# Four quarters for the last rows of a feed-forward's way down, and one low part by subtraction

## The chip, the cores and the metric

The kernel runs on one core of a Trainium2 chip. The metric is the device time of one execution in microseconds (us), the median of several runs. Engines: TensorE (PE) multiplies, VectorE (DVE) and ScalarE (ACT) work on tiles, GpSimd (POOL) issues adding transfers, SyncE (SP) issues the loads.

## What is computed

A trunk of two layers works on 512 rows of 1024 features. The first layer holds an mLSTM mixer, the second a gMLP mixer. Each mixer stands between two half-step feed-forwards (SwiGLU, hidden width 2816), and each layer ends with a gated embedding ("ple").

```python
def swiglu_ffn(x, w_gu, w_d):
    g, u = jnp.split(x @ w_gu, 2, axis=-1)
    return (jax.nn.silu(g) * u) @ w_d
...
x = layer_norm(DN_ALPHA * x + 0.5 * swiglu_ffn(x, ffn1_wgu[i], ffn1_wd[i]), ln_g[i, 0], ln_b[i, 0])
```

So there are four feed-forwards in a run, called here **A** (before the mLSTM), **B** (before the first ple), **C** (before the gMLP) and **D** (before the last ple).

## The kernel before

Float32 products are made of three products of a reduced type. Every operand is split into a high part (`hi`, a rounded copy) and a low part (`lo`, what the copy lost), and `mm3` (L388 to L390) multiplies hi by hi, hi by lo and lo by hi. A weight's high part is made by ACT (L275). Its low part comes in one of two ways: DVE subtracts (L284 at once; L290 later, "apart", inside a feed-forward), or ACT writes minus the weight (L281) and a POOL transfer adds the weight onto it (L282). Which forms take the second way is set by `by_dma`.

The class `Weights` (L50 to L360) holds the order in which weights are used. Loads go into three slots of 1 MB (`wraw`). A slot can serve as a box of two halves of 512 KB (`wbox`). `load` issues the next transfer as soon as a slot or a half is free, `fill` splits the next weights as soon as a tile for them is free. In a feed-forward `fill` leaves a weight alone that was only just loaded:

```python
if self.apart and self.ready and self.loaded_at[j] > self.clock - 2:
    return meanwhile
```

A feed-forward works through the 22 blocks of its hidden width in chunks of 2, 4, 4, 4, 4 and 4. From the third chunk on, two blocks of the way up are computed as seven products (a Strassen-like scheme). `up_forms` makes the seven weight forms r0 to r6 in place, in the boxes. r5 is the sixth. Tiles `ups` are the sums of the way up, `gps` those of the earlier chunks' way down. The last chunk's way down (`dps`, in the function `down`) needs four rows of `wd`, of 128 by 1024 each, called here rows 0 to 3. For each of four token tiles (t = 0 to 3) TensorE runs over the four rows, two halves of 512 columns and three products. DVE then adds each half to the residual (L763), takes statistics (L726 to L732) and normalises (L740, or L744 and L746). Meanwhile ACT and DVE split the normalised tile for the next stage (`xh` L639, `xl` L640), once TensorE has transposed it (`xps` L631).

The next stage begins straight behind: `sup` products of the mLSTM behind A, `pwp` of the ple behind B and D, `gvps` of the gMLP behind C. The first two weights of that stage are called n1 and n2 here. Their loads stand behind the rows' loads in SP's queue, and their splits behind the rows' splits.

Before, `add_rows` (L514) loads the four rows as two loads of 1 MB, each of two rows. The kinds in its list name the pools that the split rows take ("main", "rows", "rowsx").

Of the kernel before, what the change touches and what calls it, by code (L numbers as in the profile page):

```python
# [44 lines left out]
PLE_EXTRA = 3  # L45
UP_BY_DMA = (1, 3, 4, 5, 6)
UP_BY_DMA_2 = (1, 3, 5, 6)


class Weights:  # L50
# [307 lines left out]
def hybrid_trunk(ctx: ExitStack, tc, x, p, ln_g, ln_b, ffn1_wgu, ffn1_wd, ffn2_wgu, ffn2_wd,  # L358
# [82 lines left out]
    W = Weights(nc, raw_pool, split_pool)  # L441
# [4 lines left out]
    def kp(w):  # L446
        return w.rearrange("(kb p) c -> p kb c", p=P)
# [4 lines left out]
    def add_pairs(w, a0, b0):  # L452

        W.add((w_cols(w, a0), cols2), (w_cols(w, b0), cols2))

    def kinds_of(kind, at):
        return kind if isinstance(kind, str) else kind[at:at + 2]

    def add_rows(w, kb, n, kind="main"):
        for k in range(0, n, 2):  # L460
            W.add((kp(w)[:, kb + k:kb + k + 2, :], rows2), kind=kinds_of(kind, k))
# [9 lines left out]
    LAST = len(FFN_CHUNKS) - 1  # L471
# [3 lines left out]
    def ffn_weights(wgu, wd, name, ple=False):  # L475
        starts = [sum(FFN_CHUNKS[:c]) for c in range(LAST + 1)]

        def forms(c):
            m = FFN_CHUNKS[c] // 2

            def quarter(i, j):
                k = starts[c] + m * i
                return kp(wd)[:, k:k + m, j * 512:(j + 1) * 512]
            loads = [W.add_load(quarter(i, j), n, name) for i, j, n in ((0, 0, 2), (0, 1, 1), (1, 1, 1), (1, 0, 2))]
            return W.forms("rows", *((j, slice(None)) for j in loads))

        first = len(W.order)
        for at in range(starts[UP_FROM]):
            if at == 0 or at == starts[UP_FROM] - 1:
                W.add(*((kp(wgu)[:, :, c0:c0 + P], [slice(None)]) for c0 in (at * P, HID + at * P)))  # L490
            elif at % 2:
                add_pairs(wgu, at * P, HID + at * P)
        tiles = W.order[first:]
        del W.order[first:]
        for c, n in enumerate(FFN_CHUNKS):
            down_w = deque(forms(c - 1) if c else ())
            if c >= UP_FROM:
                products = []
                for b in range(starts[c], starts[c] + n, 2):
                    products += W.up_forms(*(W.add_load(kp(wgu)[:, k:k + 4, c0:c0 + 2 * P], 1, "box")  # L500
                                             for c0 in (b * P, HID + b * P) for k in (0, 4)),
                                            by_dma=UP_BY_DMA if b == starts[c] else UP_BY_DMA_2)
                for s, product in enumerate(products):
                    W.order.append(product)
                    if s % 2:
                        W.order.append(down_w.popleft())
                continue
            for i in range(2 * n):
                W.order.append(tiles[2 * starts[c] + i])
                if down_w:  # L510
                    W.order.append(down_w.popleft())
        if ple:
            W.add_hook("rows", lambda hi, lo: turn_p.pop()(hi, lo))
        add_rows(wd, starts[LAST], 4, ["rowsx", "rows", "main", "main"] if ple else ["main", "rows", "rowsx", "rows"])  # L514


    ML_SLOTS = (2, 3, 4, 5, 6, 7, 11)
# [71 lines left out]
    def ple_weights(i):  # L589
        add_rows(ple_wp[i], 0, 2)  # L590
        add_wide(ple_wg[i], 0, ["extra", "extra", "extra", "main"])
        add_wide(ple_wg[i], 512, ["rows", "rows", "rowsx", "rows2"])

    ffn_weights(ffn1_wgu[0], ffn1_wd[0], (0, 0))
    ml_weights()
    ffn_weights(ffn2_wgu[0], ffn2_wd[0], (0, 2), True)
    ple_weights(0)
    ffn_weights(ffn1_wgu[1], ffn1_wd[1], (1, 0))
    gm_weights()
    ffn_weights(ffn2_wgu[1], ffn2_wd[1], (1, 2), True)  # L600
# [1349 lines left out]
```

## Time and profile before

| what | value |
|---|---|
| runs | 2192.62, 2196.89, 2197.5 us; median 2196.89 |
| profiled execution | 2193.39 us, its span 2191.7 us |
| granted TensorE clock, mean | 0.999 |
| PE busy | 2170.3 us (99%) in 12821 matmuls |
| DVE busy | 1760.5 us (80%) |
| ACT busy | 1208.1 us (55%) |
| POOL busy | 226.3 us (10%) |

The span is the time from the first to the last record of the profiled execution. The rest of its time lies around it. TensorE is busy nearly all the time, so a change of the time is a change of what TensorE waits for, or of the rate at which it works. In the timeline an entry in brackets is the idle time of the engine before the instruction, and what ended it.

### The profile page before, as it was taken

The numbers are of one execution on the slowest core, as the hardware profiler recorded it, in microseconds if no ns is written. First come the engines' busy times: TensorE is split into PE (matmuls) and PEld (weight loads), VectorE is DVE, ScalarE is ACT, GpSimd is POOL, SyncE is SP. The second block draws the span as 40 slices with busy tenths as digits, with TensorE's granted clock in tenths as the row PEclk, the third lists the DMA queues.
The fourth block names the chain that finished last, engine by engine and source line by source line (L and its number), as shares of the span: only waits on it lengthen the run. The fifth ranks groups of instructions, "written<-read, shape, count | busy, mean of one in ns | idle before, by whom it ended". The sixth has DMA issues, their size and how long they took to land.

```text
span 2191.7 us, 32537 instructions
## 1 busy us (share of the span) xinstructions
PE 2170.3 (99%) x12821; PEld 1922.0 (88%) x12821; DVE 1760.5 (80%) x2532; ACT 1208.1 (55%) x1668; POOL 226.3 (10%) x279
## 2 busy tenths in 40 slices
PE   9999999999999999999999999999999999999998
PEld 8899997888888889999888899997888888999987
DVE  5898877786767789888887998877788679988887
ACT  4576656454546445667444566655345553666642
POOL 1011100011101101111000011110001100111100
PEclk9999999999999999999999999999999999999999
DMA  6587764366857426887531587754437743777651
GB/s 187 156 204 184 172 153 136 92 154 128 155 130 154 135 81 163 200 194 172 173 125 58 153 207 186 176 145 135 144 77 140 168 135 116 179 191 179 135 183 58
DMA packets 228097, 329.46 MB, mean 150 GB/s; under 512 B 9140, under 2 KB 163892, under 8 KB 227944
## 3 DMA queue, kind: packets, MB, share of 16 engines
q1 hardware_dynamic: 169104, 211.83, 29.8%
q0 software_dynamic: 52224, 100.86, 27.5%
q10 hardware_dynamic: 6616, 14.69, 1.9%
q8 instruction: 101, 1.65, 0.3%
q14 instruction: 52, 0.43, 0.1%
HBM read 224.58 MB, written 2.11 MB: 103 GB/s over the span
## 4 chain that ended last, share of the span: by engine, by line
PE 78%; DVE 11%; issue 4%; ACT 4%; DMA 3%; SPq 0%; POOL 0%; DVEq 0%; ACTq 0%; POOLq 0%
PE ups L390 7%; PE ups L388 7%; PE ups L389 7%; PE gps L388 6%; PE gps L389 6%; PE gps L390 6%; DMA wlo<-wbox 2%; PE dps L389 2%; PE dps L390 2%; PE dps L388 2%; DVE wlo L290 2%; PE fps L388 2%; PE fps L389 1%; PE fps L390 1%; ACT whi L275 1%
## 5 line engine op out<-in xcount | busy, mean ns | idle before, releaser
L275 ACT ACTIVATE whi<-wbox 128x1024 fp32r<-128x1024 f32 x224 | 235.7, 1054 | 242.2 <-DVE wbox L141 96.9
L390 PE MATMUL ups<-xh,wlo 128*128 128x256 f32 x1024 | 290.3, 284 | 3.2 <-DMA wlo<-wbox 3.2
L388 PE MATMUL ups<-xh,whi 128*128 128x256 f32 x1024 | 289.9, 283 | 0.0
L389 PE MATMUL ups<-xl,whi 128*128 128x256 f32 x1024 | 289.7, 283 | 0.0
L275 ACT ACTIVATE whi<-wraw 128x1024 fp32r<-128x1024 f32 (+1 forms) x212 | 217.3, 1046 | 96.7 <-DVE wraw L119 22.6
L388 PE MATMUL gps<-whi,fhi 128*128 128x512 f32 x644 | 253.0, 393 | 0.4
L389 PE MATMUL gps<-wlo,fhi 128*128 128x512 f32 x644 | 252.2, 392 | 0.0
L390 PE MATMUL gps<-whi,flo 128*128 128x512 f32 x644 | 251.4, 390 | 0.0
L282 POOL DMA_DIRECT2D wlo<-wbox x144 | 122.2, 848 | 1076.8 <-ACT wlo L281 705.0
L763 DVE TENSOR_TENSOR xt<-xt,gps 128x512 f32<-128x512 f32 x302 | 194.9, 680 | 26.7 <-PE gps L390 26.7
L284 DVE TENSOR_TENSOR wlo<-wraw,whi 128x1024 fp32r<-128x1024 f32 (+1 forms) x140 | 167.6, 1214 | 41.8 <-ACT whi L275 40.9
L390 PEld LDWEIGHTS ups<-xh,wlo 128*128 128x128 f32 x1024 | 196.2, 192 | 4.3 <-DMA wlo<-wbox 4.2
L388 PEld LDWEIGHTS ups<-xh,whi 128*128 128x128 f32 x1024 | 196.1, 192 | 3.8 <-ACT us L1085 1.6
L389 PEld LDWEIGHTS ups<-xl,whi 128*128 128x128 f32 x1024 | 196.1, 192 | 2.3
L275 ACT ACTIVATE whi<-wquarter 128x1024 fp32r<-128x1024 f32 (+1 forms) x140 | 135.3, 966 | 77.0 <-DVE wquarter L119 28.9
L281 ACT ACTIVATE wlo<-wbox 128x1024 fp32r<-128x1024 f32 x144 | 150.4, 1044 | 0.0
L390 PEld LDWEIGHTS gps<-whi,flo 128*128 128x128 f32 x644 | 120.9, 188 | 26.9
L388 PEld LDWEIGHTS gps<-whi,fhi 128*128 128x128 f32 x644 | 121.3, 188 | 23.9 <-issue 1.6
L389 PEld LDWEIGHTS gps<-wlo,fhi 128*128 128x128 f32 x644 | 121.3, 188 | 21.6
L944 DVE TENSOR_TENSOR flo<-h,fhi 128x512 fp32r<-128x512 f32 (+1 forms) x140 | 88.5, 635 | 57.6 <-ACT fhi L941 57.0
L290 DVE TENSOR_TENSOR wlo<-wquarter,whi 128x1024 fp32r<-128x1024 f32 x104 | 126.6, 1218 | 0.0
L388 PE MATMUL fps<-xh,whi 128*128 128x512 f32 x288 | 112.2, 390 | 0.0
(365 smaller groups left out, 5822.4 us busy)
## 6 DMA issues: line engine op xcount, KB each, us to landing
wlo<-wbox POOLq DMA_DIRECT2D x144, 512.0 KB, 5.8
wbox<-in_ffn_wgu_dram SPq DMA_DIRECT2D x128, 512.0 KB, 4.9
wquarter<-in_ffn_wd_dram SPq DMA_DIRECT2D x64, 512.0 KB, 5.8
wraw<-in_ml_w_in_dram SPq DMA_DIRECT2D x24, 1024.0 KB, 5.8
wlo<-wraw POOLq DMA_DIRECT2D x48, 512.0 KB, 6.4
wraw<-in_ffn_wgu_dram SPq DMA_DIRECT2D x15, 1024.0 KB, 6.0
wraw<-in_gm_w_in_dram SPq DMA_DIRECT2D x15, 1024.0 KB, 5.6
wraw<-in_ffn_wgu_dram SPq DMA_DIRECT2D x17, 512.0 KB, 4.8
```

The costliest lines, as they stand in the source:

```text
L275: self.nc.scalar.activation(hi[:, s], src[:, s], AF.Copy)
L281: self.nc.scalar.activation(lo[:, s], src[:, s], AF.Copy, scale=-1.0)
L282: self.nc.gpsimd.dma_start(lo[:, s], src[:, s], accum_op=OP.add)
L284: self.nc.vector.tensor_sub(lo[:, s], src[:, s], hi[:, s].bitcast(F32))
L290: self.nc.vector.tensor_sub(lo, src, hi.bitcast(F32))
L388: mm(ps, st[0], mv[0], start=start, stop=False, skip_group_check=more)
L389: mm(ps, st[0], mv[1], start=False, stop=False, skip_group_check=more)
L390: mm(ps, st[1], mv[0], start=False, stop=stop, skip_group_check=more)
L763: vec.tensor_add(dst, dst, ps)
L944: vec.tensor_sub(lo, src, hi.bitcast(F32))
```

## The change

The second pair of the last chunk makes r5's low part by subtraction on DVE. The four rows are loaded one by one, as halves of boxes. In a feed-forward that ends in a ple the second row's tile comes from the pool "main" and the third row's from "rows", the other way round than before.

```diff
+UP_BY_DMA_LAST = (1, 3, 6)
...
-                                            by_dma=UP_BY_DMA if b == starts[c] else UP_BY_DMA_2)
+                                            by_dma=UP_BY_DMA if b == starts[c] else UP_BY_DMA_2 if c < LAST else UP_BY_DMA_LAST)
...
-        add_rows(wd, starts[LAST], 4, ["rowsx", "rows", "main", "main"] if ple else ["main", "rows", "rowsx", "rows"])
+        for k, kind in enumerate(["rowsx", "main", "rows", "main"] if ple else ["main", "rows", "rowsx", "rows"]):
+            at = starts[LAST] + k
+            j = W.add_load(kp(wd)[:, at:at + 1, :], 1, "box")
+            W.order.append((kind, (j,), lambda j=j: (W.raws[j], (j,))))
```

The added lines shift the code: L290 of before is L291 of the change, L284 is L285, L740 is L744, L744 and L746 are L748 and L750, L763 is L767, L640 is L644, L1088 and L1104 are L1092 and L1108.

The order of TensorE's instructions stays as it was. Three places of DVE's order follow, before and then after.

The first place is the end of the last chunk in A, behind the last additions of `gps`. The three L290 are row 3, n1 and n2; the single L291 is row 3.

```order
L763 TENSOR_TENSOR xt<-xt,gps 128x512 x2
L290 TENSOR_TENSOR wlo<-wraw,whi 128x1024 x3
L763 TENSOR_TENSOR xt<-xt,dps 128x512
```

```order
L767 TENSOR_TENSOR xt<-xt,gps 128x512 x2
L291 TENSOR_TENSOR wlo<-wbox,whi 128x1024
L767 TENSOR_TENSOR xt<-xt,dps 128x512
```

The low parts of n1 and n2 are gone from this place. C changes here in the same way.

The second place is the end of the way down in A, from the statistics of the last token tile on, ahead of the mLSTM. Before, the four L284 are the weights behind n2.

```order
L730 BN_AGGR mv<-st 128x2
L732 TENSOR_SCALAR rs<-mv 128x1
L740 TENSOR_SCALAR xt<-xt,mv,rs 128x1024
L640 TENSOR_TENSOR xl<-xf,xh 128x4x128 x2
L284 TENSOR_TENSOR wlo<-wraw,whi 128x1024 x4
```

```order
L736 TENSOR_SCALAR rs<-mv 128x1
L744 TENSOR_SCALAR xt<-xt,mv,rs 128x1024
L285 TENSOR_TENSOR wlo<-wraw,whi 128x1024 x6
L644 TENSOR_TENSOR xl<-xf,xh 128x4x128 x4
```

The six L285 are n1, n2 and the four behind them, now ahead of the splits of x. In C the low parts of n1 and n2 go to a like place, one token tile sooner (behind the `xl` of t = 1, ahead of the L767 of t = 3).

The third place is B, from the gating of the last pair to the first addition of `dps` (D reads the same). Before, the single L290 is row 0, the five are rows 1, 2, 3, n1 and n2; after, the first two are rows 0 and 1, the second two rows 2 and 3.

```order
L1088 TENSOR_TENSOR us<-us,ups 128x512
L290 TENSOR_TENSOR wlo<-wraw,whi 128x1024
L1104 SCALAR_TENSOR_TENSOR us<-us 128x512
...
L763 TENSOR_TENSOR xt<-xt,gps 128x512 x2
L290 TENSOR_TENSOR wlo<-wraw,whi 128x1024 x5
L763 TENSOR_TENSOR xt<-xt,dps 128x512
```

```order
L1092 TENSOR_TENSOR us<-us,ups 128x512
L291 TENSOR_TENSOR wlo<-wbox,whi 128x1024 x2
L1108 SCALAR_TENSOR_TENSOR us<-us 128x512
...
L767 TENSOR_TENSOR xt<-xt,gps 128x512 x2
L291 TENSOR_TENSOR wlo<-wbox,whi 128x1024 x2
L767 TENSOR_TENSOR xt<-xt,dps 128x512
```

Here the low parts of n1 and n2 come behind the tile t = 2's L750, in a group of four L285 where before there was a group of two L284, ahead of the last tile's residual. ACT makes the high parts of n1 and n2 later as well, behind the splits of the second token tile (t = 1): in A in a group of six, ahead of the splits of t = 2 and t = 3, in B, C and D in a group of four where there was a group of two. Per feed-forward ACT has one instruction less (L281), POOL one adding transfer less (35 for 36), DVE one subtraction more. SP issues four loads of 512 KB where it issued two of 1 MB.

## Rows read from the trace of the kernel before

**Rows 1.** The waits of TensorE over the span: total, times, longest.

```profile
PE dps L389 <- DVE wlo L290: 4.8, 4, 1.6
PE ups L390 <- DMA wlo<-wbox: 3.9, 6, 1.0
PE sup L866 <- ACT xh L639: 1.1, 2, 0.8
```

**Rows 2.** The timeline of PE at the end of A: start, duration, what, idle before.

```profile
319.35 0.39 PE L390 MATMUL ups<-xh,wlo 128*128 128x256 f32 x1 [1.04 <-DMA wlo<-wbox]
...
333.92 0.50 PE L389 MATMUL dps<-wlo,wquarter 128*128 128x512 f32 x1 [1.60 <-DVE wlo L290]
...
353.97 0.28 PE L866 MATMUL sup<-xh,wlo 128*128 128x256 f32 x1
354.09 0.28 PE L866 MATMUL sup<-xh,whi 128*128 128x256 f32 x1
```

**Rows 3.** The timeline of DVE at the end of A.

```profile
322.29 0.69 DVE L1088 TENSOR_TENSOR us<-us,ups 128x512 f32<-128x512 f32 x1 [1.81 <-PE ups L390]
...
326.32 1.23 DVE L290 TENSOR_TENSOR wlo<-wraw,whi 128x1024 fp32r<-128x1024 f32 x1 [2.21 <-ACT whi L275]
...
332.64 3.49 DVE L290 TENSOR_TENSOR wlo<-wraw,whi 128x1024 fp32r<-128x1024 f32 x3
...
357.70 0.81 DVE L740 TENSOR_SCALAR xt<-xt,mv,rs 128x1024 f32<-128x1024 f32 x1 [0.66 <-POOL rs L733]
358.43 1.29 DVE L640 TENSOR_TENSOR xl<-xf,xh 128x512 fp32r<-128x512 f32 x2
```

**Rows 4.** The timeline of ACT in A: the third row's high part.

```profile
325.23 1.06 ACT L275 ACTIVATE whi<-wraw 128x1024 fp32r<-128x1024 f32 x1 [6.00 <-DMA wraw<-in_ffn_wd_dram]
```

**Rows 5.** The timeline of PE at the end of B.

```profile
1071.74 0.39 PE L390 MATMUL ups<-xh,wlo 128*128 128x256 f32 x1 [1.00 <-DMA wlo<-wbox]
...
1082.86 0.50 PE L389 MATMUL dps<-wlo,wquarter 128*128 128x512 f32 x1 [0.89 <-DVE wlo L290]
...
1105.00 0.39 PE L388 MATMUL pwp<-whi 128*128 128x512 f32 x1
1105.23 0.39 PE L389 MATMUL pwp<-wlo,whi 128*128 128x512 f32 x1
```

**Rows 6.** The timeline of DVE at the end of B.

```profile
1087.26 0.68 DVE L763 TENSOR_TENSOR xt<-xt,dps 128x512 f32<-128x512 f32 x1
...
1106.82 2.35 DVE L284 TENSOR_TENSOR wlo<-wraw,whi 128x1024 fp32r<-128x1024 f32 x2
```

**Rows 7.** The timeline of PE at the end of C.

```profile
1472.09 0.38 PE L390 MATMUL ups<-xh,wlo 128*128 128x256 f32 x1 [0.64 <-DMA wlo<-wbox]
...
1486.37 0.50 PE L389 MATMUL dps<-wlo,wquarter 128*128 128x512 f32 x1 [1.46 <-DVE wlo L290]
...
1506.08 0.39 PE L389 MATMUL gvps<-wlo,xh 128*128 128x512 f32 x1
```

**Rows 8.** The timeline of ACT at the end of C.

```profile
1505.59 1.04 ACT L275 ACTIVATE whi<-wraw 128x1024 fp32r<-128x1024 f32 x1
```

**Rows 9.** The timelines of PE and DVE at the end of D.

```profile
2126.32 0.39 PE L389 MATMUL pwp<-wlo,whi 128*128 128x512 f32 x1
2127.96 2.35 DVE L284 TENSOR_TENSOR wlo<-wraw,whi 128x1024 fp32r<-128x1024 f32 x2
```

**Rows 10.** The last matmul of the run, in the timeline of PE.

```profile
2182.95 0.28 PE L390 MATMUL gps<-whi,xl 128*128 128x256 f32 x1
```

**Rows 11.** Windows behind it: length, busy PE, PEld, DVE, ACT, POOL, PEclk, DMA, GB/s.

```profile
2184.00:2185.00 1.00, 0.00 (x0) 0.00 (x0) 0.79 (x2) 0.14 (x1) 0.00 (x0) 1.00 0.00 0
...
2186.00:2187.00 1.00, 0.00 (x0) 0.00 (x0) 1.00 (x3) 0.00 (x0) 0.85 (x1) 0.50 0.00 0
```

**Rows 12.** The timeline of PE at the start of the run.

```profile
1.43 3.36 PE L1903 MATMUL warm<-ident 128*128 128x128 f32 x16 [1.43 <-POOL ident masks.py:199]
4.91 1.09 PE L631 MATMUL xps<-ident,xt 128*128 128x128 f32 x8
```

## The prediction

> **What bounds the kernel now.** I read the times by engine first. TensorE is busy for 99% of the span, so there is no second engine whose load sets the end: time is gained or lost only where TensorE waits, or where its clock falls. The waits of TensorE come next, and they are few [rows 1]. Two of them touch what is changed: four waits of `dps` for a low part from DVE (4.8 us in all), and waits of `ups` for an adding transfer (six, 3.9 us, of which three are r5's). The timelines of the four feed-forwards then show what is late.
>
> In A, `ups` waits for r5's low part, which a POOL transfer adds up (1.04) [rows 2]. Fourteen microseconds on, `dps` waits for row 3's low part (1.60) [rows 2]. The reason lies on ACT: the high part of row 2 waits 6.00 us for the second load of two rows [rows 4]. Behind it ACT's `silu` of the last pair is held, and on DVE row 2's low part and the whole gating (326.32) [rows 3]. B has the r5 wait and a `dps` wait [rows 5], C has both [rows 7], D has the `dps` wait of B but no r5 wait.
>
> A wait takes more from TensorE than the bracket says, since the profile models a matmul's end. Matmuls of 256 columns start 0.12 apart and are drawn 0.28 long (the two `sup`) [rows 2], those of 512 columns start 0.23 apart and are drawn 0.39 long (the two `pwp`) [rows 5]; where one is drawn 0.50 long ahead of a `dps` wait, 0.27 is to be added. So a wait costs its bracket and 0.16, or 0.27 where I say so.
>
> **The change part by part.**
>
> *r5 by subtraction.* ACT loses one instruction of 1.05 and POOL one transfer per feed-forward; neither is waited for elsewhere. The waits go: 1.04 + 0.16 = 1.20 in A, 1.16 in B, 0.80 in C, nothing in D. DVE gets one subtraction of 1.22. It has an idle stretch of 1.81 just ahead of 322.29 [rows 3] to hide it; if that were gone, the gating would come 1.14 later.
>
> *Four quarters.* Rows 0, 1 and 2 no longer wait for a whole slot. In A the gating on DVE could then follow row 1's low part at once: row 2's starts at 322.29 + 0.69 + 1.22 = 324.20 at the latest where it was 326.32, 2.12 sooner, and all that follows with it. Row 3's low part, the first of the three at 332.64, ends at 332.64 − 1.20 − 2.12 + 1.22 = 330.54. TensorE will want it at 333.92 − 1.87 − 1.20 = 330.85. It is in time by 0.3 only. So 1.87 goes in A, and in the same way 1.46 + 0.16 = 1.62 in C. In B and D the first row that is late is row 1; it is now ready ahead of the gating, but that pushes the gating 1.14 back, and row 2's low part is late in its place: 1.16 goes and 0.89 comes, −0.27 each.
>
> *The first two weights of the next stage.* This is the part that speaks against the change. Before, the low parts of n1 and n2 were made right behind row 3's, some 20 us ahead of their use. A quarter's buffer comes free later than half of a load's did, the loads of n1 and n2 are issued later, and the rule that leaves a fresh load alone sends their splits past the whole way down. What is queued ahead of them on DVE is then the residual chain, and that chain ends when TensorE ends.
>
> - A. The low parts come behind the last normalisation (L740). That ends at 358.43 [rows 3]; less what was gained (1.20 + 1.87 = 3.07) it is 355.36, and n1's low part ends 1.22 later, at 356.58. TensorE wants it for the second matmul of `sup`, at 353.97 − 3.07 = 350.90. Loss 5.68. Two later waits of `sup` for the last token tile are swallowed by it: 1.1 [rows 1] and twice 0.16, 1.4.
> - B. DVE is free of three low parts, and is then held only by TensorE: the first half of `dps` of the first token tile is complete with the 13th matmul behind the one that waited, 1082.86 + 13 × 0.227 + 0.39 = 1086.20, less 0.27 is 1085.93, which is 1.33 ahead of 1087.26 [rows 6]. So DVE's chain comes 1.33 + 1.16 sooner. n1's low part then starts at 1106.82 − 2.49 = 1104.33 and ends at 1105.55. TensorE wants it at 1105.23 − 1.16 − 0.27 = 1103.80. Loss 1.75. n2 is wanted three matmuls later (0.68) and comes 1.14 later: 0.46 more. Together 2.21.
> - C. ACT's high part at 1505.59 [rows 8] is now n1's. Less 0.80 + 1.62 = 2.42 it ends at 1504.21, the low part 1.22 later at 1505.43, wanted at 1506.08 − 2.42 = 1503.66 [rows 7]. Loss 1.77; n2 has cover, since n1 serves many matmuls of `gvps`.
> - D. As B without the r5 gain: 2127.96 − 1.33 + 1.22 = 2127.85, wanted at 2126.32 − 0.27 = 2126.05 [rows 9]. Loss 1.80, and 0.46 for n2: 2.26.
>
> Sums: A −1.20 − 1.87 − 1.40 + 5.68 = +1.21; B −1.16 − 0.27 + 2.21 = +0.78; C −2.42 + 1.77 = −0.65; D −0.27 + 2.26 = +1.99. Together **+3.3**: 8.6 us of waits go, 11.9 come.
>
> *The clock.* In A TensorE would stand still for 5.7 us; no wait of [rows 1] is longer than 1.6. The trace shows what standing still does at one place: the last matmul of the run ends at 2183.23 [rows 10], the granted clock is still 1.00 at 2184 and 0.50 from 2186 on [rows 11], that is 1.2 GHz for 2.4. So it falls in less than three microseconds, and A's stall is long enough. What it then costs to come back is shown nowhere behind a fall. Below, it is nothing: the clock could be back with the first matmuls. The nearest row is the start of the run, where TensorE also comes from rest: 16 small matmuls in 3.36 (0.21 each) against 8 in 1.09 (0.14) just after [rows 12], 16 × 0.07 = 1.1 us. Above, I take as much as the stall itself, 5.7 us, as if half rate lasted for twice that. I take 1.1, the nearest row.
>
> The Trainium skill ("TensorE: Matmul & The Clock Gate", section "HAM oscillation — how this bites in real kernels") describes a kernel whose TensorE waits between bursts, falls to half rate, and pays at the head of each next burst. By that rule A's stall costs more than its length; without it the sum is +3.3, which is the first rival.
>
> The sum is +3.3 + 1.1 = **+4.4 us**. On the profiled execution (2193.39) that is 2197.8. This execution lies 3.5 below the median of the runs shown (2196.89), and the three runs spread over 4.9, so against the median the forecast is 2196.9 + 4.4 = **2201.3 us**. About 0.2% (4.4 us) is what a measurement of this kernel can tell from no change; the forecast lies on that line.
>
> **The rivals.**
>
> 1. *The stalls come, the clock holds or is back at once.* +3.3, 2200.2. For it: over the whole kernel the clock stays at 1.00. Against it: [rows 11].
> 2. *DVE's tail is not held by TensorE, and n1 is in time in B, C and D* (not slower). If the three low parts taken off DVE bring its chain 3 × 1.14 sooner right to the end, n1's low part in B ends at 1106.82 − 1.16 − 3.42 + 1.22 = 1103.46, ahead of 1103.80, and the like holds in D. It decides at that point: 1.8 us sooner than I reckon. Then B, C and D give −1.43, −2.42 and −0.27, and with A's +1.21 and 1.1 the sum is −1.8: 2195.1. Against it: `dps` halves cannot be added before TensorE has made them. Were A's stall gone as well, only the gains would stay, −8.6: 2188.3, clearly faster. For that n1's low part in A would have to come 5.7 us sooner, and it stands behind L740 on DVE.
> 3. *The quarters don't do what they are for.* If row 2's quarter also comes too late (it can be issued only once r3's adding transfer has read its buffer, and 0.3 us is all that row 3 has to spare), the waits of 1.87 and 1.62 stay in A and C. n1 is late there all the same: +4.4 + 3.5 = +7.9, 2204.8.
>
> **How the numbers follow.** I give the forecast 0.52, with the clock's price between 0 and 5.7 about it: 0.36 of this is slower by over 0.2%, 0.16 within. Rival 1 has 0.20 (within), rival 2 0.09 (within) and its faster end 0.07, rival 3 0.12 (slower). That is faster 0.07, same 0.45, slower 0.48. The range goes from rival 2 (2195.0) to the upper bound of the clock's price, 2196.9 + 3.3 + 5.7 = 2205.9, which takes in rival 3; the faster end is left out, and the spread of the runs about the ends.
>
> **What would show it.** Right: the `ups` waits of r5 and the `dps` waits of A and C are gone from TensorE's list, one wait of `sup` for a DVE low part of over 5 us stands in A, waits of `pwp` and `gvps` near 1.6 stand in B, C and D, and a granted clock below 1.00 appears behind A's stall. Wrong: the longest wait stays under 2 us; or n1's low part (L285) in A starts before L744; or the `dps` waits stay, which is rival 3. The forecast is wrong as a whole if those waits sum to less than the 8.6 that goes.

## The result, and the profile after

The change took 2200.07 us (median of 8 runs, 2198.12 to 2202.06), the kernel before 2194.68 (8 runs beside them). The ratio is 1.0025, 95% interval 1.0016 to 1.0035: slower by 5.4 us. The profiled execution of the change took 2199.77, with a span of 2198.1. The span is 6.4 us above that of before, a little more than the 5.4 between the medians.

The list of what TensorE waited for, over the whole span of the change (total, times, longest), answers to [rows 1]:

```profile
PE sup L870 <- DVE wlo L285: 5.4, 2, 5.1
PE pwp L390 <- DVE wlo L285: 3.7, 3, 1.8
PE dps L390 <- DVE wlo L291: 1.6, 2, 0.8
...
PE ups L391 <- DMA wlo<-wbox: 1.1, 3, 0.5
PE gvps L390 <- DVE wlo L285: 0.8, 1, 0.8
PE gvps L389 <- ACT whi L276: 0.7, 1, 0.7
```

The `dps` waits of A and C are gone, and r5's waits with them: the longest wait of `ups` is 0.5 where it was 1.0. In their place stand waits for the first weights of the next stage, 5.1 in A, 1.8 in each of B and D, and 0.7 + 0.8 in C.

The timeline of TensorE at the end of A, of the change, answers to [rows 2]. The first `sup` matmul goes, the second needs n1's low part:

```profile
351.50 0.38 PE L870 MATMUL sup<-xh,whi 128*128 128x256 f32 x1 [0.23 <-ACT whi L276]
356.95 0.58 PE L870 MATMUL sup<-xh,wlo 128*128 128x256 f32 x1 [5.07 <-DVE wlo L285]
357.33 0.41 PE L870 MATMUL sup<-xh,whi 128*128 128x256 f32 x1
357.55 0.41 PE L870 MATMUL sup<-xh,wlo 128*128 128x256 f32 x1
```

DVE at the same place answers to [rows 3]. Row 3's low part is made alone and in time; n1's is the first of six behind L744:

```profile
329.63 1.21 DVE L291 TENSOR_TENSOR wlo<-wbox,whi 128x1024 fp32r<-128x1024 f32 x1
...
354.95 0.81 DVE L744 TENSOR_SCALAR xt<-xt,mv,rs 128x1024 f32<-128x1024 f32 x1 [0.67 <-POOL rs L737]
355.68 6.89 DVE L285 TENSOR_TENSOR wlo<-wraw,whi 128x1024 fp32r<-128x1024 f32 x6
```

Behind the wait the `sup` matmuls start 0.21 apart, where [rows 2] has 0.12. The windows of the change show why (length, busy time of PE, PEld, DVE, ACT and POOL, granted clock, DMA share, GB/s):

```profile
355.00:356.00 1.00, 0.00 (x0) 0.00 (x0) 1.00 (x2) 1.00 (x2) 0.00 (x0) 1.00 0.00 0
356.00:357.00 1.00, 0.05 (x1) 0.05 (x1) 1.00 (x2) 1.00 (x4) 0.00 (x0) 0.75 0.00 0
357.00:358.00 1.00, 1.00 (x5) 1.00 (x6) 1.00 (x2) 0.97 (x3) 0.00 (x0) 0.50 0.00 0
358.00:359.00 1.00, 1.00 (x6) 1.00 (x6) 1.00 (x2) 0.22 (x1) 0.00 (x0) 0.50 0.00 0
359.00:360.00 1.00, 1.00 (x7) 1.00 (x6) 1.00 (x2) 0.00 (x0) 0.00 (x0) 0.54 0.87 111
360.00:361.00 1.00, 1.00 (x11) 1.00 (x10) 1.00 (x2) 0.21 (x1) 0.00 (x0) 1.00 0.93 350
```

The clock falls to 0.50 (1.2 GHz for 2.4) near the end of A's wait and is back at 1.00 by 360. In D it falls too, behind a wait of only 1.8 and some 0.7 us after TensorE has gone on, which I had not foreseen. The timeline of TensorE there, and its windows, of the change:

```profile
2130.72 0.50 PE L390 MATMUL pwp<-wlo,whi 128*128 128x512 f32 x1 [1.77 <-DVE wlo L285]
...
2132.88 0.63 PE L389 MATMUL pwp<-whi 128*128 128x512 f32 x1
2133.30 0.63 PE L390 MATMUL pwp<-wlo,whi 128*128 128x512 f32 x1
```

```profile
2132.00:2133.00 1.00, 1.00 (x3) 0.81 (x4) 1.00 (x2) 0.00 (x0) 0.00 (x0) 0.50 0.24 18
2133.00:2134.00 1.00, 1.00 (x4) 0.81 (x3) 1.00 (x2) 0.60 (x1) 0.00 (x0) 0.50 0.77 186
2134.00:2135.00 1.00, 1.00 (x4) 0.77 (x4) 0.97 (x3) 0.00 (x0) 0.00 (x0) 0.57 1.03 397
```

Both traces hold the same 12821 matmuls in the same order, so the time can be followed matmul by matmul: the start of one in the profile of the change less its start in the profile of before. The table gives this shift ahead of and behind each feed-forward's end, and the steps in it.

```
      shift ahead  shift behind  difference  forecast   its steps
A        +0.59        +2.82        +2.23     +1.21 +1.1   r5 -1.20, row 3 -1.88, sup +5.72, half rate +1.4, late xh -1.19, small steps -0.6
B        +2.98        +4.04        +1.06     +0.78        r5 -1.16, dps -1.16 and +0.95, pwp +1.95 and +0.33
C        +4.34        +3.73        -0.61     -0.65        r5 -0.81, dps -1.62, gvps +0.83 and +1.03
D        +2.77        +6.38        +3.61     +1.99        dps -1.16 and +0.95, pwp +1.94 and +0.34, clock +1.5
```

The four differences make +6.3 of the 6.4 us. Between the feed-forwards the shift drifts by up to 1 us either way.

### The profile page after: what moved, and what is told of

Same layout as the page of the kernel before. It is cut to its first block, busy times and chain, and to the rows that moved or that the text cites. A ratio compares the mean times of both kernels' runs of the same rounds, so it can differ in the third digit from the quotient of the medians.

```text
span 2198.1 us, 32548 instructions
## 1 busy us (share of the span) xinstructions
PE 2172.9 (99%) x12821; PEld 1924.1 (88%) x12821; DVE 1765.3 (80%) x2536; ACT 1203.7 (55%) x1664; POOL 223.5 (10%) x275
## 5 line engine op out<-in xcount | busy, mean ns | idle before, releaser
L276 ACT ACTIVATE whi<-wbox 128x1024 fp32r<-128x1024 f32 x240 | 251.9, 1054 | 247.9 <-DVE wbox L142 97.1
L276 ACT ACTIVATE whi<-wraw 128x1024 fp32r<-128x1024 f32 (+1 forms) x196 | 200.7, 1045 | 79.8 <-DVE wraw L120 22.6
L767 DVE TENSOR_TENSOR xt<-xt,gps 128x512 f32<-128x512 f32 x302 | 195.0, 680 | 25.8 <-PE gps L391 25.8
L285 DVE TENSOR_TENSOR wlo<-wraw,whi 128x1024 fp32r<-128x1024 f32 (+1 forms) x148 | 176.7, 1214 | 42.2 <-ACT whi L276 41.4
L291 DVE TENSOR_TENSOR wlo<-wquarter,whi 128x1024 fp32r<-128x1024 f32 x104 | 126.7, 1218 | 0.0
```

The source lines that it names most:

```text
L276: self.nc.scalar.activation(hi[:, s], src[:, s], AF.Copy)
L285: self.nc.vector.tensor_sub(lo[:, s], src[:, s], hi[:, s].bitcast(F32))
L291: self.nc.vector.tensor_sub(lo, src, hi.bitcast(F32))
L767: vec.tensor_add(dst, dst, ps)
```

## The experiments

**Theory 1**, from the prediction: the time goes into the late splits of n1 and n2, and into the clock that falls in those waits; the gains on r5 and on the rows are real. **Theory 2**, a rival: not the splits but the loads of n1 and n2, issued later, are late. Two smaller questions go with them: what half rate costs by itself, and which part of the change brought which gain.

**The splits put back (e1_early).**

```diff
-                if self.apart and self.ready and self.loaded_at[j] > self.clock - 2:
+                if self.apart and self.ready and self.loads[j][1] != "raw" and self.loaded_at[j] > self.clock - 2:
```

> The change, but the rule that leaves a freshly loaded weight alone no longer holds for whole raw loads, so the first weights of the next stage are split right behind the feed-forward's last row again. Theory 1 (the time went into the late splits of n1 and n2, and into the clock that falls in their waits): the waits of sup, pwp and gvps for a low part go, the gains on r5 and the rows stay, the clock stays at 1.00 until the end: 7 to 8.6 us under the kernel before, that is 12 to 14 under the change. Theory 2 (the loads of n1 and n2, issued later, are what is late): the splits only wait for their loads at the new place, hold up the residual chain on DVE there, and the time stays within 3 us of the change's.

It took 2184.07 us, ratio 0.9947 (0.9934 to 0.9959): 10.4 us under the kernel before, 15 to 16 under the change. Its loads stand in the same order as the change's. TensorE's waits of this run:

```profile
PE dps L390 <- DVE wlo L291: 1.6, 2, 0.8
...
PE ups L391 <- DMA wlo<-wbox: 0.5, 2, 0.3
...
PE sup L870 <- DVE wlo L285: 0.2, 1, 0.2
PE sup L870 <- ACT whi L276: 0.2, 1, 0.2
```

The waits for n1 and n2 are gone, and the clock stays at 1.00 to the end. DVE makes the low parts of n1, n2 and the weight behind them at 329.77, in one piece and without a wait, so their loads had landed:

```profile
328.64 1.22 DVE L291 TENSOR_TENSOR wlo<-wbox,whi 128x1024 fp32r<-128x1024 f32 x1
329.77 3.49 DVE L291 TENSOR_TENSOR wlo<-wraw,whi 128x1024 fp32r<-128x1024 f32 x3
333.18 0.68 DVE L767 TENSOR_TENSOR xt<-xt,dps 128x512 f32<-128x512 f32 x1
```

Theory 2 falls here. The trace of the change speaks against it too. One load of 1 MB holds n1 and n2. In A it is the first of the three in the lines below (SP's queue, before and then the change; the second number runs to the end of the third's issue):

```profile
321.93 12.33 SPq L239 DMA_DIRECT2D wraw<-in_ml_w_in_dram  x3
```

```profile
318.17 13.07 SPq L240 DMA_DIRECT2D wraw<-in_ml_w_in_dram  x3
```

In A the change issues it 3.8 us sooner, and it lands at 324.51 where before had 328.81, some 31 us ahead of the split at 355.68. In C it is issued 0.5 later and lands 0.8 sooner. In B and D it is issued 4.0 and 5.0 later, but lands only 0.3 and 0.2 later. So the load is nowhere what the split waits for. The rule that leaves a fresh load alone compares counts of steps in the building of the program (`loaded_at` and `clock`), not times on the chip. That is how a load that lands sooner can still count as fresh.

The gain is 2 us larger than I had put it. Between the two profiles it is 10.6, of which the four ends give 9.5: 8.5 in the named waits, among them 1.2 for the two late `xh` waits of [rows 1], which are gone too, and the rest in small steps. What lies between the ends I don't explain. The new rule on the kernel before, without the quarters, was not run.

**The late splits alone, on the kernel before (e5_before_late).** The mirror image: no quarter, no subtraction, only a rule that keeps `fill` in a feed-forward from splitting the next stage's weights.

```diff
+            if self.apart and self.ready and js and self.loads[js[0]][1] == "raw" and js[0] not in self.own:
+                return meanwhile
             for j in js or ():
...
+        own = len(W.loads)
         add_rows(wd, starts[LAST], 4, ["rowsx", "rows", "main", "main"] if ple else ["main", "rows", "rowsx", "rows"])
+        W.own.update(range(own, len(W.loads)))
```

> The kernel before, with nothing of the change but its side effect: the weights of the next stage are not split before the feed-forward's way down, so DVE's and ACT's order has n1 and n2 just where the change has them. Theory 1: this alone brings waits of 5 us for sup in A, about 2 in B and D for pwp and 1.8 in C for gvps, a fall of the clock behind A's, in all 11 to 13 us above the kernel before. Theory 2 (it is the later loads, not the later splits, that cost): the loads are issued as before, so the time stays within 2 us of the kernel before.

2209.36 us, ratio 1.0063 (1.005 to 1.0075): 14.4 us above the kernel before. TensorE's waits of this run are the change's new ones and before's old ones side by side:

```profile
PE sup L871 <- DVE wlo L287: 5.4, 2, 5.1
PE dps L392 <- DVE wlo L293: 5.0, 4, 1.6
PE pwp L392 <- DVE wlo L287: 3.8, 3, 1.8
PE ups L393 <- DMA wlo<-wbox: 3.7, 7, 1.1
```

The profiled execution of this run is the slowest of its five (2211.29); its span is 17.9 us above that of before. The new waits cost 11.2 of these by the steps of the shift (5.98 in A, 2.29 in B, 1.86 in C, 2.30 in D, less the 1.2 that A swallows later). The clock falls four times, and that is nearly all of the rest, 1.5 to 1.7 each by the same steps: once in each of A, B and D behind the waits for n1, and once more in A, behind the `dps` wait of [rows 2], though the clock held behind the same wait in the profile of before. One window of this run behind that `dps` wait:

```profile
334.00:335.00 1.00, 1.00 (x4) 0.78 (x3) 0.69 (x2) 0.00 (x0) 0.00 (x0) 0.50 0.48 57
```

I had put the run at 11 to 13 us with one fall. The mean clock is 0.995 in the profiled execution and 0.996 or 0.997 in the other four, so the median of 14.4 holds fewer falls than the profile.

**The clock by itself (e2_nofall).** The change, with matmuls whose result is overwritten put into the waits of A and D, so that TensorE doesn't stand still there.

```diff
+            for _ in range(again):
+                mm(ps[:, :256], w[0][:, 0], xh[:, 0, :256], start=True, stop=True)
             low_last(w, ps, 0, 256)
...
-                    banks.extend(up_staged())
+                    banks.extend(up_staged(again=40))
...
                         ps = up_bank("pwp")
+                        for _ in range(8 if last and not t and not half else 0):
+                            mm(ps, ph[:, 0, :P], ws[0][0][:, 0, :512], start=True, stop=True)
```

> The change, with TensorE kept at work in the two waits behind which the clock fell: 40 repeats of the first sup matmul in A (40 x 0.12 = 4.8 us, the wait is 5.1 long) and 8 repeats of the first pwp matmul in D (8 x 0.23 = 1.8, the wait is 1.8). The repeats are overwritten by the true first matmul. Theory 1 (half rate behind the wait is a price of its own, about 1.2 us in A and 1.5 us in D): no window of 0.50 before the end, 2.5 to 3 us under the change. Rival (what follows the wait is limited by DVE and ACT anyway, so half rate costs nothing): no fall of the clock, and within 0.5 us of the change.

2197.89 us, ratio 1.0014 (1.0005 to 1.0023), 2.2 under the change's median. The timeline of TensorE in A, of this run:

```profile
351.61 5.05 PE L885 MATMUL sup<-xh,whi 128*128 128x256 f32 x40 [0.23 <-ACT whi L276]
356.49 0.28 PE L870 MATMUL sup<-xh,whi 128*128 128x256 f32 x1
357.07 0.39 PE L870 MATMUL sup<-xh,wlo 128*128 128x256 f32 x1 [0.30 <-DVE wlo L285]
357.30 0.28 PE L870 MATMUL sup<-xh,whi 128*128 128x256 f32 x1
357.41 0.28 PE L870 MATMUL sup<-xh,wlo 128*128 128x256 f32 x1
```

The second matmul of the true group waits for the same low part as in the change, until 357.07 where that has 356.95. But now the matmuls behind it start 0.12 apart, and no window is at 0.50 before the end. The window of this run that answers to one of 0.50 in the change:

```profile
357.00:358.00 1.00, 0.93 (x7) 0.93 (x8) 1.00 (x2) 0.97 (x3) 0.00 (x0) 1.00 0.00 0
```

By the matched matmuls the run is 0.12 behind the change at that point and 1.18 ahead of it some 25 matmuls on: half rate cost 1.3 us in A. In D it is 0.39 ahead before and 1.77 after: 1.4 us. These are prices of the fall alone, on top of the waits. The sum of 2.7 is what I had put; of A's part 0.8 was lost again in small steps between A and D, so the run as a whole gained 2.2, below the forecast of 2.5 to 3. The rival (half rate costs nothing) falls.

**Each part alone.** r5's subtraction on the kernel before (e3_r5only):

```diff
+UP_BY_DMA_LAST = (1, 3, 6)
...
-                                            by_dma=UP_BY_DMA if b == starts[c] else UP_BY_DMA_2)
+                                            by_dma=UP_BY_DMA if b == starts[c] else UP_BY_DMA_2 if c < LAST else UP_BY_DMA_LAST)
```

> The kernel before with r5's subtraction alone, the rows loaded as before. Theory 1: the ups waits of r5 go in A, B and C, 3.2 us under the kernel before (1.20, 1.16, 0.80), the dps waits stay. Rival (the row's load of 2 MB competes with r5's adding transfer, so without that transfer the rows land sooner too): 4 to 5 us under it, the dps waits of A and C shrink.

2189.34 us, ratio 0.9972 (0.9961 to 0.9983): 5.2 under the kernel before, at the rival's side, and the `dps` waits of A and C are gone with it, which theory 1 had kept. (Between the two profiles it is 3.5, of which the four ends give 2.9; the rest of the 5.2 I can't place.) Why is to be read from the chain of waits of the kernel before, around A's last pair (start, length, what):

```profile
310.85 8.45 DMA wlo<-wbox
...
319.44 5.77 DMA wraw<-in_ffn_wd_dram
```

The transfer at 310.85 makes r5's low part. It takes 8.45 us, and the second load of two rows starts when it has landed: that load's slot is the one that holds r5. In B, C and D as well the second load goes out 0.1 us behind the landing of r5's transfer. So r5's wait of [rows 2] and row 3's wait 14 us later have one cause. SP's two row loads, before and then in this run (start of the first, from it to the end of the second's issue):

```profile
310.59 9.21 SPq L239 DMA_DIRECT2D wraw<-in_ffn_wd_dram  x2
```

```profile
310.69 2.59 SPq L240 DMA_DIRECT2D wraw<-in_ffn_wd_dram  x2
```

Both loads are out within 2.6 us instead of 9.2. But TensorE's waits of this run have a new one, for r6's transfer, which now runs beside both loads:

```profile
PE ups L391 <- DMA wlo<-wbox: 4.6, 7, 1.2
...
PE dps L390 <- DVE wlo L291: 1.5, 2, 0.8
```

It steps the shift by +1.38 in A, +0.90 in B, +1.22 in C and +0.91 in D. So the subtraction alone moves a good part of the wait on to the next transfer.

The quarters and the order of tiles without the subtraction (e4_rowsonly, whose edit is the change with `UP_BY_DMA_2` for all second pairs):

> The change without r5's subtraction (its low part by the adding transfer, as before). Theory 1: the r5 waits of A, B and C come back, 3.2 us above the change, about 8.5 us above the kernel before. Rival (r5's transfer was late only because of the 2 MB of rows issued beside it; with quarters it isn't): within 1 us of the change.

2199.4 us, ratio 1.002 (1.0011 to 1.0029): no different from the change. r5's wait did not come back; the waits of this run have

```profile
PE ups L391 <- DMA wlo<-wbox: 0.3, 1, 0.3
```

The rival holds. The quarters go out from 307.77 on, the first of them ahead of r5's transfer (310.32), and land in 3.4 us (median). The adding transfers of r5 and r6 in that stretch (305 to 325) took, from issue to landing, in the kernel before, in e3_r5only (r6's alone), in this run and in the change (r6's alone):

```profile
wlo<-wbox POOLq DMA_DIRECT2D x2, 512.0 KB, 8.3
```

```profile
wlo<-wbox POOLq DMA_DIRECT2D x1, 512.0 KB, 9.6
```

```profile
wlo<-wbox POOLq DMA_DIRECT2D x2, 512.0 KB, 5.6
```

```profile
wlo<-wbox POOLq DMA_DIRECT2D x1, 512.0 KB, 4.5
```

With the early splits it is the same (e6_early_r5dma, e1_early with `UP_BY_DMA_2`):

> The run with the early splits (e1_early), but r5's low part by the adding transfer, as before. If the quarters alone end r5's wait (as the run with the quarters alone showed): within 1 us of e1_early. If r5's subtraction is worth its 3.2 us: 3 us above it.

2183.93 us, ratio 0.995 (0.9937 to 0.9964), against 2184.07 with the subtraction. Once the rows come in quarters, r5's subtraction is worth nothing that these runs can tell.

**The order of tiles (e7_early_kinds).**

```diff
-        for k, kind in enumerate(["rowsx", "main", "rows", "main"] if ple else ["main", "rows", "rowsx", "rows"]):
+        for k, kind in enumerate(["rowsx", "rows", "main", "main"] if ple else ["main", "rows", "rowsx", "rows"]):
```

> e1_early with the tiles of rows 1 and 2 taken in the old order in B and D (main and rows not swapped). By my sum the swap is worth 0.27 in each of B and D: 0.5 us above e1_early, with a dps wait of about 0.9 for row 1 where e1_early has 0.8 for row 2. If the swap matters more (row 1 no longer late): above by 2 us; if it does harm: below.

2183.45 us, ratio 0.9948 (0.9935 to 0.996): no difference in the medians. In the trace row 1's wait comes back (+1.17 in B and in D) and row 2's goes (−0.95): 0.22 each, where I had said 0.27. The order of tiles moves a wait from one row to the next.

**The remaining `dps` waits (e8_early_swap).**

```diff
+                if c == LAST:
+                    W.lows(2)
                 group.add()
                 W.lows()
```

> e1_early with two of the low parts made ahead of the last two additions of gps on DVE, not behind them, in each feed-forward. The additions take 1.28, row 2's low part in B and D is late by 0.8: both dps waits go, 1.9 us under e1_early (0.95 each). Rival (the additions free the banks of gps and feed the residual chain, which then ends later by as much as it gains): within 0.5 us.

2183.91 us, ratio 0.995 (0.9937 to 0.9962): as e1_early. The `dps` waits are gone (−0.85 in B and in D), but behind them the transposes now wait for the residual chain, as TensorE's timeline in B has it:

```profile
1085.97 1.29 PE L635 MATMUL xps<-ident,xt 128*128 128x128 f32 x8 [0.16 <-DVE xt L750]
```

By the shift two such places give back 0.5 to 0.6 each. The rival was right: in either order DVE has the same work ahead of the same end, and TensorE waits for it at the rows or at the transposes.

## Why the prediction was right, and where not

It forecast 2201.3 us, 4.4 above; measured are 2200.07 and 5.4 above, within the range. The side given the largest chance (slower by over 0.2%) came, though by little: the interval of 0.16 to 0.35% takes in the 0.2%. That the time itself came so close is in part luck. It was added to the median of three runs (2196.89), which lies 2.2 above that of the eight (2194.68), and the change was put 1.0 too low. The mechanism is what speaks for the prediction: the difference of each feed-forward's end came within 0.3 us in A, B and C. (The lower end of the range is 2195.1 by rival 2's sum and 2195.0 where the range is given; nothing rests on it.)

*The first two weights of the next stage.* Right, and shown twice, by taking the late splits away (−15 us against the change) and by adding them alone (+14 us). The sizes held too: A 5.68 forecast and 5.72 stepped, with the 1.40 swallowed later measured at 1.19; B 1.75 + 0.46 against 1.95 + 0.33; C 1.77 against 0.83 + 1.03; D 1.80 + 0.46 against 1.94 + 0.34. The reading behind it, that n1's low part is queued behind a chain on DVE that ends when TensorE ends, could be made from the order and the rows of before, since DVE keeps its order. One reason given for it was wrong as a matter of time: "the loads of n1 and n2 are issued later" does not hold in A, where the load goes out 3.8 us sooner. It is later only in the steps of the building of the program, which the rule counts.

*The clock.* The term of 1.1 in A measured 1.3. What failed is that A's stall ("In A TensorE would stand still for 5.7 us") was taken as the one place where the clock would fall: D's wait of 1.8 brought a fall as well, another 1.4 us, and that is most of the difference between 4.4 and the 6.4 of the profiles. Rival 1 (the clock holds) is excluded by the windows and by e2_nofall.

*r5 by subtraction.* Here the mechanism failed, though not the sum. I booked 1.20, 1.16 and 0.80 to the subtraction (of ACT's instruction and POOL's transfer it says that "neither is waited for elsewhere"), and 1.87 and 1.62 to the quarters. These steps of the shift came as forecast, but for another reason. The second row load does wait for the transfer, whose source lies in the slot that the load takes: one cause for both waits. That the transfer in its turn was slow because of the row loads beside it is the likely reading (8.3 and 9.6 us with loads of 1 MB beside, 5.6 and 4.5 with quarters), but size and time of issue changed together. Each half of the change ends both waits: the quarters alone (e4_rowsonly), and the subtraction alone, which opens a third (e3_r5only). The sum was right since the gains were taken once each; as a sum of two independent parts it was wrong.

*Four quarters.* Row 3 was in time, as forecast, and in B and D row 2 is late in row 1's place (0.79 read, 0.89 forecast). Rival 3 (the rows stay late) did not happen. Rival 2 (DVE's tail is not held by TensorE) fell in B, C and D: n1 was late there by 1.95, 1.86 and 1.94, close to the sums that have the tail held by TensorE.

## What to carry to other kernels

A change to when a buffer comes free also moves whatever is loaded into it next. If a rule defers work on what has just arrived, a step or two in the order of the program at the load can become twenty microseconds at the split, behind a chain that ends only when the bottleneck engine does. So follow the first operands of the next stage through every queue before booking a gain, and when two waits vanish together, look for the one transfer that holds both. Here the gains of the change were real: with the deferral rule mended for whole loads it is 10.4 us faster than the kernel before, not 5.4 slower.

## What the runs showed of the hardware

The granted clock fell behind waits of quite different lengths. It fell behind 5.1 us in A, and behind 1.8 in D of the change but not behind the like 1.8 in B; in e4_rowsonly not in D; in e5_before_late in B and D, and behind a `dps` wait of 1.6 which the kernel before goes through at 1.00. What decides it at the short waits stays open. Whether a fall comes seems to differ between executions of one kernel too, since the mean clock does. Of the change's eight runs four list a mean clock of 0.997 and took 2198.1 to 2199.8 us, four list 0.996 and took 2200.4 to 2202.1. Of 23 runs of the kernel before, 16 list 0.999 (2193.1 to 2195.6) and seven 0.998 (2195.1 to 2197.6). So much of the spread of a kernel's times goes with the clock, and one profile shows only which falls came in that execution.

A fall cost 1.3 and 1.4 us where it was taken away. It is not a fixed price: it goes with how long TensorE works at the low level. In A of the change TensorE worked at 0.50 from 356.95 to 359.9, some 3.0 us. In A of e4_rowsonly, behind a wait of the same 5.07, it did so from 355.83 to 360.4, some 4.6 us, and the shift grew by about 2.1 there where the change has 1.4. The end of that stretch, of e4_rowsonly:

```profile
360.00:361.00 1.00, 1.00 (x9) 1.00 (x8) 1.00 (x2) 0.71 (x3) 0.00 (x0) 0.78 1.05 403
```

An adding transfer of 512 KB took 8.45 us beside a row load of 1 MB and another adding transfer, 9.6 beside two row loads, and the two in that stretch took 5.6 (median) where the rows came as 512 KB and earlier. Both differ between those runs, size and time of issue; which of them counts was not tried.
